# Round counts as one bit mask and one maximum, and the late expert rounds as one loop over the groups, in a two-layer encoder kernel

## The chip, the core and the metric

The kernel runs on one core of a Trainium2 chip. Its engines are TensorE (PE; its weight loads are PEld), VectorE (DVE), ScalarE (ACT), GpSimd (POOL) and SyncE (SP, which here issues nearly all weight transfers). Each engine has a sequencer of its own (PEq, DVEq, ...) that fetches its instructions, takes its branches, and loads its registers. The metric is the device time of one execution in microseconds (us).

## What is computed

Two layers. Each mixes 256 tokens of width 1024 through three branches and one output projection, normalises, and then sends every token to two of 32 experts:

```
x = layer_norm(alpha * x + merged @ w_out[l])
lg = x @ w_rg + b_rg                       # 4 expert groups: the best one
le_sel = the 8 expert logits of that group # the best two experts
h = silu(x @ w_gate_e) * (x @ w_up_e)      # per expert, D_EXPERT = 256
moe_out = (h * weights) @ w_down_e
x = layer_norm(alpha * x + moe_out)
```

How many tokens an expert gets is known only at run time: 16 on the average, and more or less by the data.

## The kernel before, in words

**Stages.** In each layer the mixer comes first: large products whose fp32 weights are split in two (lines 335 and 336), with TensorE busy nearly throughout. Then comes the router, a chain of small DVE and ACT operations, and then the experts. Layer 0's experts run from about 292 to 496 us of the profile, layer 1's from about 785 to 996 us.

**Experts.** The 32 experts are worked in NG = 8 groups of four; this is a grouping of the kernel, not the router's. Each expert has 32 columns of a group's 128, so a group's first round takes up to 32 tokens of each of its experts. For each group `g`, `pick` and `gather` bring the tokens into `xs` by products with a selection matrix `M.S`, eight `columns` steps multiply by the gate and up weights (one 1 MB unit `("gu", l, g, k)` each), and `hidden`, `turn` and four more `columns` steps (`("dn", l, g, k)`) follow. `combine` adds the result to four accumulators.

**More tokens than 32.** Inside the group loop a second round stands under `tc.If(nrv[g] > 0)`: three such branches in group 0 and two in the others around the gate and up products (line 1421), and two around the down products (line 1465), 33 in a layer. An `If` whose condition is false is a branch over its body and a small wait on each engine. Third and later rounds, for an expert with over 64 tokens, stand in `last_rounds` (line 1307), which group 5 calls after its second `columns` step (line 1412). It holds `more_rounds` written out eight times, once for each group, each with a loop over that group's rounds, and all under one `tc.If(nrv[NG] > 1)` (line 1310). In this execution no expert has over 64 tokens, so that branch passes over everything in both layers. In layer 1 groups 2 and 3 have an expert with over 32 tokens and run their second rounds; in layer 0 no group does.

**Counts.** `rounds` (line 1316) turns the counts in `rb_[:, 64:96]` into nine numbers of further rounds, one per group and one over all, by a scale, a rounding by adding and subtracting MAGIC, and a cast to int32. `values_load_multi_w_load_instructions` (line 1392) then has every engine load the nine into registers, with one TENSOR_LOAD. On PE it stands between the last of the WARM = 5 rows of products with zeros (four accumulators each, which start the accumulators and keep the engine at work) and the gather of group 0.

**Weights.** Weight units go through rings of buffers (`Stream`): about 23 units of 1 MB fit ahead. A unit's buffer is given back by `st.done`, in program order, and SP issues the next transfer into it once the engines are past the last use. So transfers stop when all rings are full, and go on when the first group's products give back buffers.

Of the kernel before, what the change touches and what calls it, by code (L numbers as in the profile page):

```python
# [10 lines left out]
F32 = mybir.dt.float32  # L11
F32R = mybir.dt.float32r
BF16 = mybir.dt.bfloat16
I32 = mybir.dt.int32
# [10 lines left out]
NG = 8  # L25
# [169 lines left out]
def emit(nc, tc, dram, out):  # L195
    from contextlib import ExitStack
    ctx = ExitStack()
    with ctx:
# [116 lines left out]
        V.tensor_scalar(ramp[:, 0], iota[:, :64], -1.0, 65.0, op0=OP.mult, op1=OP.add)  # L315
        magic = cp.tile([128, 1], F32, name="magic")
        V.memset(magic, MAGIC)
        hpi = cp.tile([128, 1], F32, name="hpi")
        V.memset(hpi, math.pi / 2)

# [160 lines left out]
        for l in range(L):  # L481
# [685 lines left out]
            e32 = rt([2, 2])  # L1167
            V.tensor_scalar(e32, eid, 32.0, 1.0, op0=OP.mult, op1=OP.add)

            def slots_of(rank, to=None, first=False, beside=lambda: None):  # L1170

                (va, vb, sl), slg = to or ([rt([2, 2]) for _ in range(3)], rt([2, 2, NG]))
                V.tensor_add(va, e32, rank)
                beside()
                if first:
                    V.scalar_tensor_tensor(sl, rank, 32.0, va, op0=OP.is_lt, op1=OP.mult)
                else:
                    V.scalar_tensor_tensor(vb, rank, 32.0, va, op0=OP.is_lt, op1=OP.mult)
                    V.scalar_tensor_tensor(sl, rank, 0.0, vb, op0=OP.is_ge, op1=OP.mult)
                beside()  # L1180
                g128 = iota0[:, 0:NG].unsqueeze(1).to_broadcast([128, 4, NG])
                sl4 = sl.rearrange("p t k -> p (t k)").unsqueeze(2).to_broadcast([128, 4, NG])
                V.scalar_tensor_tensor(slg.rearrange("p t k g -> p (t k) g"), g128, -128.0, sl4, op0=OP.mult, op1=OP.add)
                return slg
# [11 lines left out]
            class X:  # L1196
# [3 lines left out]
                sg, h = l1[:, 0:256], l1[:, 256:512]  # L1200
                hT = cut(sg, [2, 128])
                wv = rt([1])
                rx = rt([2, 2])
                slots = [rt([2, 2]) for _ in range(3)], rt([2, 2, NG])
                bank = pps.tile([128, 512], F32, name="xbank", bufs=1)

# [73 lines left out]
                    for t in range(2):  # L1280
                        mm(accs[t][hf], ST[:, 128 * t:128 * t + 128], yp, False, False)

            def more_rounds(g, y, wf):

                V.tensor_copy(X.rx, rk1)
                with tc.For_i(1, nrv[g], 1):
                    V.tensor_scalar(X.rx, X.rx, -32.0, None, op0=OP.add)
                    pick(g, slots_of(X.rx, X.slots), X)
                    place_back(X, X.bank)
                    for k in (0, 4):  # L1290
                        gather(NG, X.S, X.xs, range(k, k + 4), X.bank)
                    def fetch(src):
                        def w(e):
                            P.dma_start(wf, src[:, 512 * e:512 * e + 512])
                            return wf
                        return w

                    for k in range(8):
                        columns(X.bank, X.xs[k // 4][:, k % 4], fetch(dram["w_gu"][l, g * 8 + k]), k == 0, k == 7)
                    hidden(X.bank, X)  # L1300
                    turn(X, X.bank)
                    for hf in range(2):
                        for f in range(2):
                            columns(X.bank, X.hT[:, f, :], fetch(dram["w_dn"][l, g * 4 + 2 * hf + f]), f == 0, f == 1)
                        combine(X.ST, parts_of(X.bank, y), hf)

            def last_rounds():
                x_rows()
                y = parts_tiles("wl", "wl")
                with tc.If(nrv[NG] > 1):  # L1310
                    for i in range(NG):
                        more_rounds(i, y, l0)

            accs = [[acc_bank() for _ in range(2)] for _ in range(2)]

            def rounds():

                nx = rt([NG + 1])
                V.tensor_reduce(nx[:, :NG], rb_[:, 64:96].rearrange("p (g e) -> p g e", g=NG), axis=AX.X, op=OP.max)
                V.tensor_reduce(nx[:, NG:], rb_[:, 64:96], axis=AX.X, op=OP.max)  # L1320
                yield
                V.tensor_scalar(nx, nx, 1.0 / 32.0, -1.0 / 32.0 - 0.484375, op0=OP.mult, op1=OP.add)
                yield
                V.tensor_scalar(nx, nx, MAGIC, None, op0=OP.add)
                yield
                V.tensor_scalar(nx, nx, MAGIC, 0.0, op0=OP.subtract, op1=OP.max)
                yield
                nxi = rt([NG + 1], I32)
                V.tensor_copy(nxi, nx)
                yield nxi  # L1330

            def weights():
# [47 lines left out]
            with tc.manual_schedule(engines={mybir.EngineType.DVE}):  # L1380

                more = rounds()
                rp = rt([2, 2, 32], t=l1)
                V.tensor_mul(rp, eoh, rb_[:, :64].rearrange("p (t e) -> p t e", t=2).unsqueeze(2).to_broadcast([128, 2, 2, 32]))
                next(more)
                rk = rt([2, 2])
                V.tensor_reduce(rk, rp, axis=AX.X, op=OP.add)
                next(more)
                slg0 = slots_of(rk, first=True, beside=lambda: next(more))
                nxi = next(more)  # L1390
                next(nxt)
                nrv = nc.values_load_multi_w_load_instructions(
                    nxi[0:1, :], min_val=0, max_val=7,
                    skip_runtime_bounds_check_because="an expert has at most 256 tokens, in rounds of 32")[1]
                next(nxt)
                xs = next(nxt)
                rk1 = rt([2, 2])
                V.tensor_scalar(rk1, rk, -32.0, None, op0=OP.add)
                slg1 = slots_of(rk1)
                for _ in wts:  # L1400
                    pass
            for g in range(NG):
                hb = ps_bank()
                for ks in ((0,), (1, 2, 3), (4, 5, 6, 7)) if g == 0 else ((0, 1, 2, 3), (4, 5, 6, 7)):
# [13 lines left out]
                        x_rows()  # L1418
                    if 0 in ks or 7 in ks:
                        xb = ps_bank()  # L1420
                    with tc.If(nrv[g] > 0):
                        if 0 in ks:
                            pick(g, slg1, X)
                            gather(g, X.S, X.xs, range(4), xb)
                            gather(g, X.S, X.xs, range(4, 8), X.bank)
                        for k in ks:
                            columns(X.bank, X.xs[k // 4][:, k % 4], W[k], k == 0, k == 7)
                        if 7 in ks:
                            place_back(X, xb)
                            hidden(X.bank, X)  # L1430
# [21 lines left out]
                for hf in range(2):  # L1452
# [9 lines left out]
                    y = parts_of(yb, y4[hf])  # L1462
                    if g == NG - 1 and hf == 1 and l + 1 == L:
                        last_sums(0)
                    with tc.If(nrv[g] > 0):  # L1465
                        if hf == 0:
                            turn(X, X.bank)
                        for f in range(2):
                            columns(X.bank, X.hT[:, f, :], W[f], f == 0, f == 1)
                        combine(X.ST, parts_of(X.bank, y4[1 - hf]), hf)  # L1470
# [37 lines left out]
```

## Time and profile before

| what | us |
|---|---|
| median of three runs | 1006.58 |
| the three runs | 1005.23, 1006.58, 1011.27 |
| profiled execution, its own time | 1009.82 |
| its span, first to last instruction | 1008.0 |
| PE busy in the span | 892.0 |
| DVE, ACT busy | 577.7, 480.5 |
| instruction fetches, queue q8 | 81 packets, 1.33 MB |

The span is the time between the first and the last recorded instruction; what lies around it is 1.8 us here. A timeline row gives start, duration, engine, line, operation, the tiles written and read, and the count of merged instructions; the bracket at its end is the idle time of the engine just before and what ended it. A product of fp32 data is two weight loads and two products in the trace, so eight `mm` calls show as x16. Register, branch and semaphore instructions are not counted as busy; their durations are seen under the line that issues them.

### The profile page before, as it was taken

Reading aid. Unit: us, or ns where it says so; the run is one execution under the profiler, and the core shown is the slowest. Engines: PE = TensorE matmul, PEld = TensorE weight load, DVE = VectorE, ACT = ScalarE, POOL = GpSimd, SP = SyncE. Lnnn points to the kernel's source line nnn. Section 1 sums busy time; section 2 is a strip of 40 time slices with the busy share of each in tenths; the row PEclk is TensorE's granted clock in tenths of the full one; section 3 lists DMA queues with packets and bytes.
Section 4 is the critical chain, followed back from the end, with each engine's and each line's share of the span. In section 5 each row is a group of like instructions: output and inputs, shape, how many; then the busy total and the mean of one; then the engine's idle time right before and its main releaser. Section 6 shows DMA issues by size and latency. Waiting matters only on the chain. (4 is left out here: it accounts for less than half of the span.)

```text
span 1008.0 us, 19488 instructions
## 1 busy us (share of the span) xinstructions
PE 892.0 (88%) x7718; PEld 662.1 (66%) x7718; DVE 577.7 (57%) x1231; ACT 480.5 (48%) x994; POOL 28.3 (3%) x60
## 2 busy tenths in 40 slices
PE   6899999998989999666797999999899889899793
PEld 6898998988864454212496988998897445444341
DVE  7979798885753212110598998998675331211115
ACT  6876967757532211001389787866664211111112
POOL 3000100000000000001000000000000000000001
PEclk9999999999989999989898999999999989999897
DMA  8573354449759999999984335434788699999991
GB/s 302 214 288 137 101 215 168 169 151 411 315 205 381 418 414 416 412 419 416 354 317 188 98 143 196 184 130 164 282 319 333 235 418 418 418 418 411 414 413 67
DMA packets 48084, 289.06 MB, mean 287 GB/s; under 512 B 5328, under 2 KB 6608, under 8 KB 16080
## 3 DMA queue, kind: packets, MB, share of 16 engines
q1 hardware_dynamic: 47808, 286.26, 72.0%
q8 instruction: 81, 1.33, 0.5%
q10 hardware_dynamic: 144, 1.05, 0.3%
q14 instruction: 51, 0.42, 0.1%
HBM read 286.24 MB, written 1.05 MB: 285 GB/s over the span
## 5 line engine op out<-in xcount | busy, mean ns | idle before, releaser
L336 DVE TENSOR_TENSOR wl<-ringA,wh 128x512 fp32r<-128x512 f32 x280 | 190.0, 692 | 58.5 <-ACT wh L335 55.1
L335 ACT ACTIVATE wh<-ringA 128x512 fp32r<-128x512 f32 x280 | 170.7, 629 | 91.1 <-PE acc L215 76.4
L215 PE MATMUL acc<-xh,wh 128*128 128x256 f32 x576 | 168.6, 295 | 11.7 <-ACT wh L335 11.7
L215 PE MATMUL acc<-xh,wl 128*128 128x256 f32 x576 | 168.0, 292 | 6.1 <-DVE wl L336 5.8
L215 PE MATMUL acc<-xl,wh 128*128 128x256 f32 x576 | 166.7, 290 | 0.0
L215 PEld LDWEIGHTS acc<-xh,wh 128*128 128x128 f32 x576 | 113.2, 198 | 14.6 <-ACT wh L335 12.8
L215 PEld LDWEIGHTS acc<-xh,wl 128*128 128x128 f32 x576 | 113.8, 198 | 8.4 <-DVE wl L336 7.1
L215 PEld LDWEIGHTS acc<-xl,wh 128*128 128x128 f32 x576 | 113.5, 197 | 0.5 <-issue 0.4
L215 PEld LDWEIGHTS ps<-late,xt 128*128 128x128 f32 x544 | 69.8, 208 | 26.6 <-issue 22.0
L215 PE MATMUL ps<-late,xt 128*128 128x128 f32 x544 | 74.4, 295 | 13.7 <-issue 5.9
L215 PE MATMUL acc<-yh,wh 128*128 128x256 f32 x224 | 65.1, 293 | 7.2 <-ACT yh L1038 5.4
L215 PE MATMUL acc<-yh,wl 128*128 128x256 f32 x224 | 64.3, 288 | 0.9 <-DVE wl L336 0.9
L215 PE MATMUL acc<-yl,wh 128*128 128x256 f32 x224 | 64.0, 288 | 0.0
L1275 DVE TENSOR_TENSOR y<-ps,y 128x512 fp32r<-128x512 f32 x32 | 22.1, 692 | 62.1 <-ACTq L1465 51.5
L1274 ACT ACTIVATE y<-ps 128x512 fp32r<-128x512 f32 x32 | 19.1, 598 | 79.7 <-PE ps L215 75.9
L1219 ACT ACTIVATE late<-ps 128x256 fp32r<-128x256 f32 x18 | 6.9, 383 | 99.6 <-PE ps L215 99.6
L215 PEld LDWEIGHTS acc<-y,late 128*128 128x128 f32 x144 | 24.3, 192 | 42.1 <-issue 24.8
L215 PE MATMUL acc<-y,late 128*128 128x512 f32 x144 | 45.6, 432 | 5.8 <-ACT y L1274 3.7
L215 PEld LDWEIGHTS acc<-yh,wh 128*128 128x128 f32 x224 | 43.0, 193 | 9.7 <-ACT yh L1038 5.8
L1209 DVE TENSOR_TENSOR late<-ri,late 128x512 bf16<-128x512 f32 x18 | 12.4, 690 | 64.3 <-PE ps L215 64.1
L215 PE MATMUL ps<-ringA,xs 128*32 128x512 f32 x256 | 34.6, 655 | 14.4 <-PEq L1310 7.6
L215 PEld LDWEIGHTS acc<-yh,wl 128*128 128x128 f32 x224 | 43.4, 194 | 1.6 <-DVE wl L336 1.5
(405 smaller groups left out, 1696.5 us busy)
## 6 DMA issues: line engine op xcount, KB each, us to landing
e<-w_gu SPq DMA_DIRECT2D x34, 1024.0 KB, 9.3
ringB<-w_gu SPq DMA_DIRECT2D x32, 1024.0 KB, 16.7
ringA<-w_gu SPq DMA_DIRECT2D x32, 1024.0 KB, 15.6
ringB<-w_dn SPq DMA_DIRECT2D x31, 1024.0 KB, 16.5
ringA<-w_gate SPq DMA_DIRECT2D x24, 1024.0 KB, 4.9
e<-w_dn SPq DMA_DIRECT2D x23, 1024.0 KB, 12.6
ringA<-w_in SPq DMA_DIRECT2D x15, 1024.0 KB, 4.8
ringA<-w_br SPq DMA_DIRECT2D x12, 1024.0 KB, 4.8
```

The costliest lines, as they stand in the source:

```text
L215: PE.matmul(o, lhsT, rhs, start=start, stop=stop, skip_group_check=True)
L335: A.activation(wh, w, AF.Copy)
L336: V.tensor_sub(wl, w, wh)
L1209: V.tensor_tensor(r.S2, iota.unsqueeze(1).unsqueeze(1).to_broadcast([128, 2, 2, 128]), slg[:, :, :, g].unsqueeze(3).to_broadcast([128, 2, ...
L1219: A.activation(r.ST, b[:, 0:256], AF.Copy)
L1274: A.activation(yh, yb, AF.Copy)
L1275: V.tensor_sub(yl, yb, yh)
```

## The change

Three things, all in the expert stage, and one constant:

- `rounds` makes two numbers in place of nine: `full`, the sum of `1 << g` over the groups with an expert over 32.5 tokens (by a comparison, a product with a constant row `bits`, and a sum), and `most`, the largest count itself. Each engine's TENSOR_LOAD loads two registers.
- The 33 branches of a layer test `full & (1 << g)`, which is one register operation more on each engine ahead of each branch.
- `last_rounds` holds the body once: a loop over the eight groups with the weight addresses taken from the loop's register, and in it a loop over the rounds, whose limit comes from `most`. The slots of the group are reached by moving `X.e`, a copy of `e32`, down by 128 after each group.
- `bits` is filled by eight one-column memsets at the start of the kernel.

WARM is 5 in both kernels. The heart of the diff:

```
-                nx = rt([NG + 1])
-                V.tensor_reduce(nx[:, :NG], rb_[:, 64:96].rearrange("p (g e) -> p g e", g=NG), axis=AX.X, op=OP.max)
-                V.tensor_reduce(nx[:, NG:], rb_[:, 64:96], axis=AX.X, op=OP.max)
+                nx, gx = rt([2]), rt([NG])
+                V.tensor_reduce(gx, rb_[:, 64:96].rearrange("p (g e) -> p g e", g=NG), axis=AX.X, op=OP.max)
+                V.tensor_reduce(nx[:, 1:2], rb_[:, 64:96], axis=AX.X, op=OP.max)
                 yield
-                V.tensor_scalar(nx, nx, 1.0 / 32.0, -1.0 / 32.0 - 0.484375, op0=OP.mult, op1=OP.add)
+                V.scalar_tensor_tensor(gx, gx, 32.5, bits, op0=OP.is_gt, op1=OP.mult)
                 yield
-                V.tensor_scalar(nx, nx, MAGIC, None, op0=OP.add)
+                V.tensor_reduce(nx[:, 0:1], gx, axis=AX.X, op=OP.add)
                 yield
-                V.tensor_scalar(nx, nx, MAGIC, 0.0, op0=OP.subtract, op1=OP.max)
+                nxi = rt([2], I32)
+                V.tensor_copy(nxi, nx)
                 yield
-                nxi = rt([NG + 1], I32)
-                V.tensor_copy(nxi, nx)
                 yield nxi
...
-                nrv = nc.values_load_multi_w_load_instructions(
-                    nxi[0:1, :], min_val=0, max_val=7,
+                full, most = nc.values_load_multi_w_load_instructions(
+                    nxi[0:1, :], min_val=0, max_val=256,
...
-                    with tc.If(nrv[g] > 0):
+                    with tc.If(full & (1 << g)):
...
-                with tc.If(nrv[NG] > 1):
-                    for i in range(NG):
-                        more_rounds(i, y, l0)
+                with tc.If(most > 64):
+                    V.tensor_copy(X.e, e32)
+                    with tc.For_i(0, NG, 1) as g:
+                        V.tensor_copy(X.rx, rk1)
+                        with tc.For_i(1, ((most + 31) >> 5) - 1, 1):
+                            V.tensor_scalar(X.rx, X.rx, -32.0, None, op0=OP.add)
+                            pick(0, slots_of(X.rx, X.slots, e=X.e), X)
...
+                        V.tensor_scalar(X.e, X.e, -128.0, None, op0=OP.add)
```

On DVE, layer 0, between the first use of the rank products and the gather matrix (`late` is the scratch tile that holds the counts, the slots and `M.S`), the program before has

```order
L1387 TENSOR_REDUCE late<-late 128x4
L1322 TENSOR_SCALAR late<-late 128x9
L1173 TENSOR_TENSOR late<-late 128x4
L1324 TENSOR_SCALAR late<-late 128x9
L1176 SCALAR_TENSOR_TENSOR late<-late 128x4
L1326 TENSOR_SCALAR late<-late 128x9
L1183 SCALAR_TENSOR_TENSOR late<-ri,late 128x32
L1329 CAST late<-late 128x9
L1209 TENSOR_TENSOR late<-ri,late 128x512
L1211 TENSOR_TENSOR late<-late 128x256
L1392 TENSOR_LOAD late
```

and the changed program, at the same place, has

```order
L1391 TENSOR_REDUCE late<-late 128x4
L1327 SCALAR_TENSOR_TENSOR late<-late,bits 128x8
L1177 TENSOR_TENSOR late<-late 128x4
L1329 TENSOR_REDUCE late<-late 128x1
L1180 SCALAR_TENSOR_TENSOR late<-late 128x4
L1332 CAST late<-late 128x2
L1187 SCALAR_TENSOR_TENSOR late<-ri,late 128x32
L1213 TENSOR_TENSOR late<-ri,late 128x512
L1215 TENSOR_TENSOR late<-late 128x256
L1396 TENSOR_LOAD late
```

One operation fewer stands there, and the cast that the register loads wait for comes one pair earlier, ahead of the slots' last operation; the two that make `M.S` stay behind that one.

On PE, at the call of `last_rounds` in group 5, the program before goes on like this, the rows from L1286 to the next L1286 being repeated eight times:

```order
L1310 COMPARE_AND_BRANCH
L1286 COMPARE_AND_BRANCH
L1286 UNCONDITIONAL_BRANCH x2
L177 BRANCH_PREFETCH_HINT
L1216 MATMUL xbank<-ident,late 128x128 x2
```

and the changed program has, with the body in it once:

```order
L1298 COMPARE_AND_BRANCH
L1300 COMPARE_AND_BRANCH
L1300 UNCONDITIONAL_BRANCH x2
L177 BRANCH_PREFETCH_HINT
L1302 REGISTER_ALU x3
L1302 COMPARE_AND_BRANCH
L1302 UNCONDITIONAL_BRANCH x2
L177 BRANCH_PREFETCH_HINT
L1220 MATMUL xbank<-ident,late 128x128 x2
```

Seven of the eight bodies are gone between the branch and its target. Counted in the two built programs, with four instructions to a product of fp32 data as in the trace, PE has 24,874 instructions before and 20,598 after, and the branch passes over 2,514 before and 343 after.

## Rows read from the trace of the kernel before

**Rows 1.** The page's head, and its row on instruction fetches (queue: packets, MB).

```profile
span 1008.0 us, 19488 instructions
...
q8 instruction: 81, 1.33, 0.5%
```

**Rows 2.** Busy time by stretch: us, PE, PEld, DVE, ACT, POOL, PEclk, DMA share, GB/s.

```profile
290.00:300.00 10.00, 7.47 (x40) 6.29 (x40) 2.40 (x11) 1.26 (x3) 0.00 (x0) 0.66 0.16 44
300.00:310.00 10.00, 9.53 (x87) 4.79 (x86) 3.29 (x13) 1.62 (x5) 0.00 (x0) 1.00 0.77 305
...
780.00:790.00 10.00, 6.82 (x42) 5.14 (x41) 3.36 (x18) 3.74 (x11) 0.00 (x0) 0.83 0.32 116
...
980.00:990.00 10.00, 8.19 (x76) 2.61 (x72) 0.64 (x2) 3.07 (x6) 0.00 (x0) 1.00 0.44 179
```

**Rows 3.** Timeline of all engines, layer 0's router and first group.

```profile
289.15 0.17 DVE L1329 CAST late<-late 128x9 int32<-128x9 f32 x1
...
290.00 0.42 DVE L1211 TENSOR_TENSOR late<-late 128x256 fp32r<-128x256 bf16 x1
...
291.93 5.46 PE L215 MATMUL ps<-late,xt 128*128 128x128 f32 x24 [3.02 <-issue]
...
298.70 0.33 SPq L157 DMA_DIRECT2D e<-w_dn  x1
```

**Rows 4.** The same place in layer 1.

```profile
782.86 0.42 DVE L1211 TENSOR_TENSOR late<-late 128x256 fp32r<-128x256 bf16 x1
...
784.63 4.41 PE L215 MATMUL ps<-late,xt 128*128 128x128 f32 x24 [2.85 <-issue]
```

**Rows 5.** PE's register loads at line 1392: count, ns min/median/max, first and last start.

```profile
L1392 PEldq TENSOR_LOAD <-late x2: 2193/2275/2357, 289.4 to 782.2; - x2
```

**Rows 6.** PE timeline of layer 0 around the branch of line 1310, and near the layer's end.

```profile
410.10 3.48 PE L215 MATMUL ps<-ringA,xs 128*32 128x512 f32 x16 [4.31 <-PEq L1310]
...
415.87 1.92 PE L215 MATMUL ps<-ringA,xs 128*32 128x512 f32 x16 [1.75 <-issue]
...
420.12 1.07 PE L215 MATMUL ps<-ringD,xs 128*32 128x512 f32 x8 [1.46 <-DMA ringD<-w_gu]
...
488.40 1.57 PE L215 MATMUL ps<-e,late 128*32 128x512 f32 x8 [1.44 <-DMA e<-w_dn]
```

**Rows 7.** PE timeline of layer 1: a plain group, the branch of line 1310, the end.

```profile
912.56 1.19 PE L215 MATMUL acc<-y,late 128*128 128x512 f32 x4
...
920.16 2.02 PE L215 MATMUL ps<-late,xt 128*128 128x128 f32 x16 [0.32 <-PEq L1421]
...
931.57 1.19 PE L215 MATMUL acc<-y,late 128*128 128x512 f32 x4
936.03 3.56 PE L215 MATMUL ps<-ringA,xs 128*32 128x512 f32 x16 [3.27 <-PEq L1310]
...
941.61 0.19 PE L215 MATMUL ps<-late 128*128 128x3 bf16 x2 [1.62 <-issue]
...
943.22 3.42 PE L215 MATMUL ps<-ringD,xs 128*32 128x512 f32 x16
...
948.02 2.02 PE L215 MATMUL ps<-late,xt 128*128 128x128 f32 x16 [0.53 <-ACT late L1258]
...
991.89 1.06 PE L215 MATMUL ps<-e,late 128*32 128x512 f32 x8
```

**Rows 8.** What PE's weight loads waited for on transfers, 780 to 1008 us: total, times, longest.

```profile
PEld ps L215 <- DMA ringB<-w_dn: 0.6, 1, 0.6
...
PEld ps L215 <- DMA e<-w_dn: 0.3, 1, 0.3
```

**Rows 9.** PE's branches by line: count, ns min/median/max, first and last start.

```profile
L1310 PEldq COMPARE_BRANCH  x2: 6017/6168/6319, 403.6 to 929.8; - x2
...
L1421 PEldq COMPARE_BRANCH  x38: 70/223/4460, 296.2 to 983.0; - x38
...
L1465 PEldq COMPARE_BRANCH  x36: 73/210/422, 311.5 to 991.1; - x36
```

More of the change, by code (lines that the diff above doesn't have):

```diff
@@ L317, in emit @@
         V.memset(magic, MAGIC)
+        bits = cp.tile([128, NG], F32, name="bits")
+        for g in range(NG):
+            V.memset(bits[:, g:g + 1], float(1 << g))
         hpi = cp.tile([128, 1], F32, name="hpi")
@@ L1168, in emit, with slots_of @@
             V.tensor_scalar(e32, eid, 32.0, 1.0, op0=OP.mult, op1=OP.add)
-            def slots_of(rank, to=None, first=False, beside=lambda: None):
+            def slots_of(rank, to=None, first=False, beside=lambda: None, e=e32):
                 (va, vb, sl), slg = to or ([rt([2, 2]) for _ in range(3)], rt([2, 2, NG]))
-                V.tensor_add(va, e32, rank)
+                V.tensor_add(va, e, rank)
                 beside()
@@ L1202, in emit @@
                 wv = rt([1])
-                rx = rt([2, 2])
+                rx, e = rt([2, 2]), rt([2, 2])
                 slots = [rt([2, 2]) for _ in range(3)], rt([2, 2, NG])
@@ L1281, in combine @@
                         mm(accs[t][hf], ST[:, 128 * t:128 * t + 128], yp, False, False)
[L1283 to L1305, printed above, removed]
@@ L1307, in last_rounds, with fetch, w @@
             def last_rounds():
                 x_rows()
-                y = parts_tiles("wl", "wl")
-                with tc.If(nrv[NG] > 1):
-                    for i in range(NG):
-                        more_rounds(i, y, l0)
+                y, wf = parts_tiles("wl", "wl"), l0
+                def fetch(src):
+                    def w(e):
+                        P.dma_start(wf, src[:, 512 * e:512 * e + 512])
+                        return wf
+                    return w
+                with tc.If(most > 64):
[5 more added lines that the diff above has]
+                            pick(0, slots_of(X.rx, X.slots, e=X.e), X)
+                            place_back(X, X.bank)
+                            for k in (0, 4):
+                                gather(NG, X.S, X.xs, range(k, k + 4), X.bank)
+                            for k in range(8):
+                                columns(X.bank, X.xs[k // 4][:, k % 4], fetch(dram["w_gu"][l, g * 8 + k]), k == 0, k == 7)
+                            hidden(X.bank, X)
+                            turn(X, X.bank)
+                            for hf in range(2):
+                                for f in range(2):
+                                    columns(X.bank, X.hT[:, f, :], fetch(dram["w_dn"][l, g * 4 + 2 * hf + f]), f == 0, f == 1)
+                                combine(X.ST, parts_of(X.bank, y), hf)
+                        V.tensor_scalar(X.e, X.e, -128.0, None, op0=OP.add)
@@ L1391, in emit @@
                 next(nxt)
-                nrv = nc.values_load_multi_w_load_instructions(
-                    nxi[0:1, :], min_val=0, max_val=7,
-                    skip_runtime_bounds_check_because="an expert has at most 256 tokens, in rounds of 32")[1]
+                full, most = nc.values_load_multi_w_load_instructions(
+                    nxi[0:1, :], min_val=0, max_val=256,
+                    skip_runtime_bounds_check_because="there are eight groups, and an expert has at most 256 tokens")[1]
                 next(nxt)
@@ L1464, in emit @@
                         last_sums(0)
-                    with tc.If(nrv[g] > 0):
+                    with tc.If(full & (1 << g)):
                         if hf == 0:
```

## The prediction

> **What bounds the kernel now.** I read the page's head, then the busy time by stretch, to find where each engine and the transfers go idle; then the timeline at those places; then the register loads and branches by line. The profiled execution took 1009.82 us, 1.8 around a span of 1008.0 [rows 1] and 3.24 over the median of 1006.58. I make the sum as a difference and take it from both.
>
> The change touches only the expert stages. Each opens with a hole: from 290 to 300 us the transfers fall to a 0.16 share and from 780 to 790 to 0.32, and in just these stretches TensorE's granted clock averages 0.66 and 0.83 [rows 2]. The rings are full there, and nothing is given back before the first group's products. Layer 0 goes on transferring only when SP issues at 298.70 [rows 3].
>
> After the hole the layers differ. In layer 0 PE catches up with its weights: it waits for one at 420.12 (1.46 us), and still at 488.40 (1.44 us) [rows 6]. So layer 0's end is set by transfers, which run without a gap once restarted: a gain ahead of the restart reaches the end whole, and a PE stall in mid-layer costs nothing. In layer 1 PE, which also runs second rounds there, waits for a transfer 0.6 and 0.3 us in all [rows 8]. The transfers end near 984.4 (a 0.44 share of 980 to 990 [rows 2]), while the last down weights, which come ahead of one more 1 MB unit (about 2.5 us at the rate of these stages), are used at 991.89 [rows 7]. So there PE is the bound, about 10 us behind its last weights, and a PE stall counts in full, until some 9 us are saved.
>
> **The register loads.** PE's load of nine takes 2.19 to 2.36 us [rows 5]. In layer 0 it starts at 289.4, after the cast, and the gather starts at 291.93; its matrix `M.S` is there at 290.00 + 0.42 = 290.42 [rows 3]. So the load, not the matrix, holds PE. Two registers instead of nine: between 2/9 of 2.28, or 0.51 us, if time goes by the register, and 2.28 if it is one fixed trip. I take the first: at 0.25 us each, nine reads done one after another fit. The load then ends near 289.8 and the matrix becomes the late one, which the order leaves where it was. With 0.05 us for the hand-over the gather starts at 290.47, a gain of 1.46; in layer 1 at 782.86 + 0.42 + 0.05 = 783.33 instead of 784.63 [rows 4], a gain of 1.30. Together **2.8 us**. At the other bound only the missing DVE operation remains, at most the 0.17 of a cast per layer: 0.3. DVE's, ACT's and SP's loads shrink too, behind PE's, where nothing waits for them.
>
> [...]
>
> **The clock.** The gather's 24 products took 5.46 us in layer 0 and 4.41 in layer 1 [rows 3, 4]; 16 such products at full clock take 2.02 [rows 7], so 24 take 3.03. [...] The idle time shrinks to about 1.5 us. After an idle of 1.75 at 415.87 sixteen products ran at full speed, in 1.92 [rows 6]; after one of 1.62 at 941.61 the next sixteen took 3.42 [rows 7]. The rows point both ways, so between 0 and 2.43 + 1.38 = 3.8 I take the middle, **1.9 us**.
>
> **The jump over the late rounds.** PE's branch at line 1310 takes 6.0 to 6.3 us, the others by line 0.2 at the median [rows 9]. In layer 0 this is free, as shown. In layer 1, from the `combine` at 931.57 to the next gather at 948.02, PE needs 16.45 us; in the plain group before, from 912.56 to 920.16, it needs 7.60 [rows 7]. The jump thus costs 8.85 us: 3.27 idle, 1.64 because the next 16 products take 3.56 rather than 1.92 [rows 6, 7], and the rest, 3.9, in an aftermath without a branch: 1.62 idle at 941.61 and a second slow stretch at 943.22.
>
> Is it the length of the jump? Queue q8 fetched 81 packets of 1.33 MB, 16.4 KB each [rows 1]. PE's stream, 24,874 instructions less twice the 2,514 passed over, is 19,846, so about 67 bytes each: I read 256 instructions of 64 bytes to a packet. The idle times at 415.87 and 941.61 stand at no branch; I read them as packet borders whose packet was late. Between them the built program counts 12,281 instructions, 48 packets less 7: good to one per written loop. Counted from these borders in the changed program, layer 0's jump leaves at instruction 136 of a packet and lands at about 481, inside the next one, which was fetched ahead. Layer 1's leaves at 178 and lands at 523: 11 beyond the next packet. So I take the 6 us stall to **stay in layer 1** and vanish only in layer 0, where it was free. But layer 1 then lands at a packet's start, with some 245 instructions to run while the next is fetched, where before it landed near a packet's end. The aftermath goes, a gain of **3.9 us**. Bounds: 0, if the aftermath repeats too; 8.85, if the jump costs what short ones do.
>
> [...]
>
> **What costs nothing.** A layer has 33 more register operations on PE, one per `If`; bounds: nothing, and the shortest PE branch, 70 ns [rows 9], which makes 2.3 us in layer 1. I take nothing: PE's sequencer runs ahead of its products, so far that a 4.46 us stall at a line-1421 branch [rows 9] left 0.53 idle [rows 7]. Without that cover it is the 2.3. The eight one-column memsets stand ahead of the first input's arrival on DVE. The warm-up rows are five in both.
>
> **Sum.** 2.8 + 1.9 + 3.9 = 8.6 us: 1009.82 becomes 1001.2 under the profiler, and the median 1006.58 becomes **998.0 us**.
>
> **The rivals.** *A: the jump is short everywhere.* Layer 1 also keeps the 4.9 us of idle and slow products: 993.1. For it speaks that 343 is nearer to the 43 to 135 instructions of the other `If`s than to 2,514; against it the count, which has to be off by 11.
>
> *B: the load is one fixed trip.* Gains 0.3, no shorter idle, so no clock: 0.3 + 3.9 = 4.2, or 1002.4. Nothing in the rows speaks against it, as both loads seen are of nine.
>
> *C, on the other side: the shifted code brings packets late at other branches.* Every `If` after the change lies elsewhere in its packet, and a branch into a packet still on its way has cost up to 4.46 us [rows 9]. Where it shows on PE as the long jump does (3.27 + 1.64 = 4.9 us), one makes 1002.9, two make 1007.8, slower than before; two is the point from which it decides, and over 1% slower takes four. For it: 66 branches move. Against it: at all of line 1465's branches the stall stayed within 0.42 us [rows 9], and only PE's in layer 1 count.
>
> *D: nothing of it reaches the end.* If layer 0's gain were eaten by a later wait, 998.0 plus 2.4 (its 1.46 and half the clock term), 1000.4; the transfers' full load after the hole speaks against it.
>
> **How the numbers follow.** The forecast has 0.55: with the clock's bounds 6.7 to 10.5 us gained, 996.1 to 999.9. A has 0.18 (991.2 to 995.0 with the same bounds), B 0.12, C 0.08 (0.05 with one, 0.03 with more), D 0.07. From 992.0 to 1003.0 about 0.9 of this lies inside, its top being B or one late packet, and some 0.8 once a cause that I have not named is allowed for. A measurement of this kernel tells some 1% from no change, here 10.1 us, or 996.5. Faster by over 1%: A and the forecast's fast edge, where the clock holds in both layers, 0.28. Slower by over 1% needs four late packets, 0.03. Within 1%: 0.69.
>
> **What would show it.** PE's TENSOR_LOAD near 0.5 us, and the gather ended by DVE's `M.S` with about 1.5 us of idle ahead: the first term. Gathers of 24 products between 3.0 and 5.5 us: the second. PE's branch at the new line 1298 near 0.3 in layer 0 and near 6 us in layer 1, with no further idle at a packet border in group 5: the third; near 0.3 in both is A. I am wrong if PE's load stays at 2 us, if layer 0's end does not move with its first group, or if PE idles 3 us at an `If` of layer 1.

## The result, and the profile after

The changed kernel takes **996.6 us** (median; 995.22 to 999.33) against 1006.3 for the kernel before (1005.23 to 1011.27). The ratio is 0.9878, with a 95% interval of 0.9847 to 0.9908: 1.2% faster. 998.0 was forecast, with 992 to 1003 as the range. A second measurement of the same kernel gave 0.9902 (0.9872 to 0.9932), so the gain is 1.0 to 1.2%.

The profiled execution took 995.22 us. The page's head and its row of instruction fetches [rows 1], then busy time by stretch [rows 2]:

```profile
span 993.6 us, 19826 instructions
...
q8 instruction: 80, 1.31, 0.5%
```

```profile
290.00:300.00 10.00, 7.58 (x66) 4.56 (x64) 5.30 (x26) 2.70 (x6) 0.00 (x0) 1.00 0.54 186
...
780.00:790.00 10.00, 9.09 (x81) 5.07 (x84) 4.78 (x21) 2.11 (x5) 0.00 (x0) 1.00 0.39 116
970.00:980.00 10.00, 7.06 (x52) 2.05 (x44) 3.72 (x7) 3.54 (x6) 0.00 (x0) 1.00 0.72 296
```

In both router stages the granted clock, third from the end, is now 1.00 where it was 0.66 and 0.83. In single microseconds from 292 to 297 us it was 0.50 before: the lower clock of what follows. The timeline of layer 0's router [rows 3] and of layer 1's [rows 4], with the last warm-up products ahead:

```profile
289.07 1.17 PE L215 MATMUL acc<-zeros 128*128 128x512 f32 x4
...
290.25 0.16 DVE L1332 CAST late<-late 128x2 int32<-128x2 f32 x1
...
291.32 0.42 DVE L1215 TENSOR_TENSOR late<-late 128x256 fp32r<-128x256 bf16 x1
...
291.89 2.92 PE L215 MATMUL ps<-late,xt 128*128 128x128 f32 x24 [1.66 <-DVE late L1215]
...
295.95 0.33 SPq L157 DMA_DIRECT2D e<-w_dn  x1
```

```profile
776.81 1.17 PE L215 MATMUL acc<-zeros 128*128 128x512 f32 x4
...
779.06 0.42 DVE L1215 TENSOR_TENSOR late<-late 128x256 fp32r<-128x256 bf16 x1
...
779.63 2.92 PE L215 MATMUL ps<-late,xt 128*128 128x128 f32 x24 [1.65 <-DVE late L1215]
```

PE no longer waits for its own load (`issue`) but for the matrix of line 1215, and the 24 products take 2.92 us in both layers. PE's loads [rows 5] and its branches and register operations by line [rows 9]:

```profile
L1396 PEldq TENSOR_LOAD <-late x2: 554/638/722, 290.4 to 778.2; - x2
```

```profile
L1298 PEldq COMPARE_BRANCH  x2: 325/3166/6006, 401.3 to 920.5; - x2
...
L1425 PEldq COMPARE_BRANCH  x38: 74/224/2913, 294.6 to 968.4; - x38
L1425 PEldq ALU_OP  x34: 36/36/42, 294.5 to 968.3; - x34
```

The jump over the late rounds takes 0.33 us in layer 0 and still 6.01 in layer 1. PE's timeline there, and at the layer's end [rows 7]:

```profile
922.31 1.20 PE L215 MATMUL acc<-y,late 128*128 128x512 f32 x4
926.79 1.92 PE L215 MATMUL ps<-ringA,xs 128*32 128x512 f32 x16 [3.28 <-PEq L1298]
...
933.33 2.02 PE L215 MATMUL ps<-late,xt 128*128 128x128 f32 x16 [0.38 <-PEq L1425]
```

```profile
975.31 1.07 PE L215 MATMUL ps<-e,late 128*32 128x512 f32 x8 [0.40 <-DMA e<-w_dn]
...
977.78 1.07 PE L215 MATMUL ps<-e,late 128*32 128x512 f32 x8 [0.28 <-DMA e<-w_dn]
```

From the `combine` ahead of the jump to the next gather PE needs 11.02 us instead of 16.45, and at the end it now waits for its last down weights. Before, it used them at 991.89, 7.6 us after they had landed (at 984.3).

The spans differ by 14.4 us, more than the medians do. Followed through both timelines, after against before:

- the last warm-up products of layer 0's router start 1.33 us **later** (a stretch at the lower clock near 232 us that the trace of before does not have);
- layer 0's gather starts 1.37 us earlier after them, and takes 2.54 less;
- from there to layer 1's router it is 1.2 us less;
- layer 1's gather starts 1.20 us earlier after its warm-up products, and takes 1.49 less;
- from there to PE's last product it is 7.96 us less, of which the stretch at the jump is 5.43.

About 3 us of the rest of the last item are the same products at the lower clock in the trace of before and at the full one in this; the first of them, in PE's timeline of before, then of after:

```profile
820.91 3.75 PE L215 MATMUL ps<-late,xt 128*128 128x128 f32 x16 [3.16 <-DVE late L1211]
```

```profile
814.41 2.02 PE L215 MATMUL ps<-late,xt 128*128 128x128 f32 x16 [2.92 <-DVE late L1215]
```

### The profile page after: what moved, and what is told of

Its sections match the earlier page's. It is cut to its first block, busy times and chain, and to the rows that moved or that the text cites. A ratio compares the mean times of both kernels' runs of the same rounds, so it can differ in the third digit from the quotient of the medians.

```text
span 993.6 us, 19826 instructions
## 1 busy us (share of the span) xinstructions
PE 882.3 (89%) x7718; PEld 656.0 (66%) x7718; DVE 577.9 (58%) x1237; ACT 480.9 (48%) x994; POOL 28.3 (3%) x60
## 5 line engine op out<-in xcount | busy, mean ns | idle before, releaser
L215 PEld LDWEIGHTS ps<-late,xt 128*128 128x128 f32 x544 | 66.0, 198 | 25.1 <-issue 16.3
L215 PE MATMUL ps<-late,xt 128*128 128x128 f32 x544 | 70.4, 284 | 11.3 <-DVE late L1215 6.2
L215 PEld LDWEIGHTS acc<-yl,wh 128*128 128x128 f32 x224 | 43.8, 196 | 0.1
```

What stands on the lines that cost most here:

```text
L215: PE.matmul(o, lhsT, rhs, start=start, stop=stop, skip_group_check=True)
```

## The experiments

The registers and the loop were tried apart, then the jump's landing, the idle time ahead of the gathers, and the price of a register. "The stretch" below is always PE's time in layer 1 from the start of the `combine` ahead of the late rounds to the start of the next gather; "before" is 16.45.

**The two registers alone.** The written copies are back:

```
-                    with tc.For_i(0, NG, 1) as g:
+                    for g in range(NG):
                         with tc.For_i(1, ((most + 31) >> 5) - 1, 1):
```

> The change without its loop: two registers, but the late rounds written eight times, so that PE passes over 2,517 instructions again instead of 343. Theory (what a jump costs is set by where it lands in its packet): the gain of the load and of the gather's clock stays, 1.38 + 2.54 us in layer 0 and 1.20 + 1.49 in layer 1; the branch at the jump still takes about 6 us in both layers, but in layer 1 it lands 19 instructions into a packet instead of 215 into one, so the second idle time of 1.6 us and the second slow stretch behind it are gone all the same, and from the products before the jump to the second gather behind it PE needs 11 to 13 us as in the changed kernel, not 16.45. In all 995 to 997 us. Rival (the length of what is passed over counts): the stretch takes 16.45 again, only 6.6 us of gain remain: 999.7 us.

Measured: 0.9917 (0.9885 to 0.9948), median 999.8. PE's timeline at the jump of layer 1:

```profile
924.01 1.20 PE L215 MATMUL acc<-y,late 128*128 128x512 f32 x4
928.53 3.64 PE L215 MATMUL ps<-ringA,xs 128*32 128x512 f32 x16 [3.32 <-PEq L1298]
...
937.50 2.02 PE L215 MATMUL ps<-late,xt 128*128 128x128 f32 x16 [0.40 <-PEq L1422]
```

The trace goes with the theory: 2,517 instructions are passed over, and still the second idle time of 1.62 us and the second slow stretch [rows 7] are gone; the stretch takes 13.49. The time decides nothing: against 1006.3 the theory's 995 to 997 us are ratios of 0.989 to 0.991 and the rival's 999.7 is 0.993, and the interval holds them all, as it does the 0.9902 of the changed kernel's second measurement. Nor is the gain the registers' alone: 0.83% is 8.4 us, and the shorter stretch, which came without the loop, is 3 of them in this trace. In layer 0 the branch took 6.23 us again, and from SP's restart to layer 1's register load went 482.1 us, as with the short jump (482.2): there the stall is free.

**The loop alone.** A load of nine words again, the late rounds written once:

```
-                nxi = rt([2], I32)
+                nxi = rt([NG + 1], I32)
```

> The change without its short load: late rounds written once, but the register load again of nine words (seven of them are zeros that nobody reads). PE's instructions stand exactly where they stand in the changed kernel, so the jump of layer 1 leaves and lands at the same places. Theory: PE's load takes 2.3 us again, PE is idle some 2.8 to 3.0 us ahead of both gathers, and their 24 products take 5.4 and 4.4 us instead of 2.92; the stretch at the jump of layer 1 stays at 11.0. In all 996.6 + 6.6 = 1003 us, less what waits at transfers in the end anyway: 1001 to 1003.5. Rival (the gain of the gather came with the shorter code, not with the load): gathers at 2.92 and 997 us.

Measured: 0.9961 (0.9945 to 0.9978). The gathers of layer 0 and layer 1:

```profile
294.38 5.46 PE L215 MATMUL ps<-late,xt 128*128 128x128 f32 x24 [2.80 <-issue]
```

```profile
786.56 2.92 PE L215 MATMUL ps<-late,xt 128*128 128x128 f32 x24 [2.63 <-issue]
```

The ratio is where the expectation had it (against 1006.3, 1001 to 1003.5 us are 0.995 to 0.997). The idle times are as expected; the first gather went at the lower clock, the second, behind 2.63 us of idle, at the full one. So the clock has chance in it, and one gather of one trace decides nothing. The stretch took 12.95 us, where 11.0 was expected. The two halves give 0.83% and 0.39%, the whole 1.0 to 1.2%; but they are no sum of two parts, since the shorter stretch at the jump is in both.

**No late rounds at all.** The call of `last_rounds` is left out.

> The change, with the late rounds left out altogether (on these inputs no expert needs them): no jump at line 1298 at all. Two things differ. If PE is still the bound in layer 1, the 3.4 us that the jump still costs there (11.02 us against the 7.60 of a plain group) come off: 993 us. If the transfers have become the bound (in the changed kernel PE waits 0.40 and 0.28 us for the last down weights), nothing is gained beyond about half a microsecond: 996 to 997 us, with longer waits of PE for transfers in the last two groups of layer 1. I expect the second.

Measured: 0.9886 (0.9856 to 0.9915), 996.5 us. The stretch is 7.66 us, and nothing is gained in time. The end of layer 1:

```profile
973.56 1.07 PE L215 MATMUL ps<-e,late 128*32 128x512 f32 x8 [0.23 <-DMA e<-w_dn]
975.88 1.07 PE L215 MATMUL ps<-e,late 128*32 128x512 f32 x8 [1.25 <-DMA e<-w_dn]
...
978.35 1.06 PE L215 MATMUL ps<-e,late 128*32 128x512 f32 x8 [0.28 <-DMA e<-w_dn]
```

PE waits 1.25 us for one weight where the changed kernel waited 0.40. Its last product ends 1.6 us after the layer's last transfer, against 9.5 in the kernel before and 1.7 and 4.0 in two traces of the changed one. With PE waiting for weights, what is saved at the jump beyond that is waited out. In layer 1, as in layer 0, the transfers are the bound now, or nearly.

**The changed kernel again.**

> The changed kernel once more, to see what of its trace is steady: the ratio to the kernel before between 0.985 and 0.991 again. If the load and the idle time set the gather's clock, both gathers take 2.9 us again with 1.6 us of idle ahead. The stretch at full or lower clock elsewhere (1.3 us lost at 234 us, 3.1 gained at 820 us against the kernel before) may come and go: if it is chance, one of the two is not there this time.

Measured: 0.9902. The gather of layer 1 took 2.92 us again, that of layer 0 4.54, behind the same 1.65 us of idle. The lower clock near 232 us was there (0.59 granted from 232 to 236 us), that near 820 was not. The stretch took 13.60 us: 3.58 us of idle (3.27 before), and 16 products at the lower clock behind it (3.64). The first profile's 11.02 was the lucky one. PE's timeline at the gather of layer 0, then at the jump of layer 1:

```profile
292.92 4.54 PE L215 MATMUL ps<-late,xt 128*128 128x128 f32 x24 [1.65 <-DVE late L1215]
```

```profile
929.92 3.64 PE L215 MATMUL ps<-ringA,xs 128*32 128x512 f32 x16 [3.58 <-PEq L1298]
```

**Where the jump lands.** Products are left out of the body that never runs, so that the landing moves by a few instructions; first one, then five (`DROP` = 4, 3, then 2, 1 of four):

```
-                                combine(X.ST, parts_of(X.bank, y), hf)
+                                combine(X.ST, parts_of(X.bank, y), hf, DROP[hf])
```

> The changed kernel with one product less in the body of the late rounds (one of the eight of their combines is left out; the body does not run on these inputs): two PE instructions less in each layer, 341 passed over. By the count of packets layer 1's jump then lands 7 instructions beyond the next packet, where the changed kernel lands 11 beyond. Theory (the landing's packet decides): PE's branch in layer 1 takes about 6 us as before, and the stretch from the products ahead of the jump to the next gather 11 to 13.6 us; layer 0's branch stays at 0.33. Rival (the stall has another cause than the packet): the same here, so this run is only read beside the next one.

> The same with five of the eight combines of the late rounds' body left out: ten PE instructions less, near enough 334 passed over, and layer 1's jump lands 7 instructions inside the next packet. Theory: the branch takes 0.3 us in layer 1 too, the stretch falls to 7.7 us, as without late rounds, and in the end PE is 1.6 to 2 us behind the transfers instead of 4. Rival (343 and 334 instructions are the same to the branch): 6 us and 11 to 13.6 us as in the run with two less.

PE's branches of the two runs, one execution each:

```profile
L1299 PEldq COMPARE_BRANCH  x2: 334/3188/6043, 402.3 to 923.5; - x2
```

```profile
L1299 PEldq COMPARE_BRANCH  x2: 334/466/597, 403.6 to 923.1; - x2
```

6.04 us with the landing 7 instructions beyond the next packet, 0.60 with it 7 inside. The count of packets holds at this border to within 14 instructions. But the stretch fell only to 11.53, not to 7.7, and here the expectation was wrong. PE's timeline of the second run shows why:

```profile
924.86 1.20 PE L216 MATMUL acc<-y,late 128*128 128x512 f32 x4
926.21 1.02 PE L216 MATMUL ps<-ringA,xs 128*32 128x512 f32 x3
929.79 1.91 PE L216 MATMUL ps<-ringA,xs 128*32 128x512 f32 x13 [2.57 <-issue]
```

After three products PE reaches, by the count, the end of the packet in which it landed, and waits 2.57 us without a branch. The next packet comes only now: queue q8 moves none between 922.3, ahead of the branch, and 927.08, 3.4 us after the landing. That is the idle time of the kernel before at 941.61 [rows 7] over again. The stall had moved, not gone.

The traces also give its size. From the moment at which PE goes on in one packet (here the branch's end, 923.69) to the first instruction of the next packet, where that one is late (here 929.79), it is 6.1 us here, and 5.7 to 6.3 us in all late packets behind these jumps but one (3.7, one group earlier with six rows). In the kernel before it is 5.8 us (935.82 to 941.61). So what shows as idle time is these 6 us less what PE still finds to do in the packet where it landed.

**The late rounds' code one group earlier.** `if g == NG - 4: last_rounds()`; the landing is then at instruction 178 of its packet.

> The changed kernel with the whole of its late rounds, but with their code put one group earlier (group 4 instead of 5). Nothing is left out. By the count of packets the jumps then land at instruction 392 and 434 from the start of the packet that they leave, inside the next one in both layers. Theory: 0.3 us at both branches, the stretch at the jump 7.7 us instead of 11.0 to 13.6, and PE 1.6 to 2 us behind the transfers at the end of layer 1; as without late rounds, a ratio near 0.987 to the kernel before and about 995 to 997 us, 1 to 2 us less than the changed kernel. Rival (moving the code only moves the late packet to another branch): a branch of 3 us or more elsewhere in layer 1 and no gain, 998.

Measured: 0.9872 (0.9843 to 0.9900). The branches took 3.83 us in layer 0, where 0.3 was expected, and 0.45 in layer 1. The stretch took 8.67, and behind its end PE idled once more without a branch:

```profile
909.82 3.64 PE L215 MATMUL ps<-ringB,xs 128*32 128x512 f32 x32 [0.99 <-PEq L1425]
...
915.33 1.50 PE L215 MATMUL ps<-late,xt 128*128 128x128 f32 x12 [0.86 <-issue]
```

So the rival was right in part: late packets moved elsewhere. The next `If` of layer 1 waited 2.99 us for its packet, that of layer 0 5.30, and the 0.86 us is one more; all three ended 5.7 to 5.9 us after PE had gone on in the packet before. That would explain the 3.83 too, though no run tests it: by the count, this jump leaves its packet some 50 instructions from the start, when the next one may still be on its way. On PE the waits cost little, and layer 0's are free: from SP's restart to layer 1's register load it is 482.3 us. In time the kernel cannot be told from the changed one, as the end at the transfers lets one expect.

**The landing moved in the kernel before.** Nine registers, eight copies, three of four products left out of each `combine` in the bodies:

```
-                        combine(X.ST, parts_of(X.bank, y), hf)
+                        combine(X.ST, parts_of(X.bank, y), hf, 1)
```

> The kernel before, nine registers and eight written copies, with six of the eight combines of each copy's body left out (the bodies do not run on these inputs): 2,426 instructions are passed over instead of 2,514. By the count of packets layer 1's jump then lands 39 instructions into a packet instead of 215, and layer 0's 245 into one instead of 77. Theory (the landing decides what follows the jump): the branches still take about 6 us in both layers, but in layer 1 the idle time of 1.6 us and the slow products behind it are gone: the stretch takes 12 to 13.6 us instead of 16.45, and PE is 5 to 7 us behind the transfers at the end instead of 9.5: 3 to 4 us less, a ratio of 0.996 to 0.997, with no other part of the change in it. Rival (the number of instructions passed over counts): 2,426 is as good as 2,514, the stretch stays at 16 and the ratio at 1.000.

```profile
929.92 1.19 PE L215 MATMUL acc<-y,late 128*128 128x512 f32 x4
934.61 3.64 PE L215 MATMUL ps<-ringA,xs 128*32 128x512 f32 x16 [3.50 <-PEq L1310]
...
943.70 2.02 PE L215 MATMUL ps<-late,xt 128*128 128x128 f32 x16 [0.41 <-PEq L1421]
```

The stretch took 13.78 us with 2,426 instructions passed over: 2.67 us less, nearly all of the 2.85 that the changed kernel gains there in its second profile and half of the 5.43 in its first, with no line of the change in it. On the time it is unclear: 0.9985 (0.9962 to 1.0008), where 0.996 to 0.997 was expected; 2.67 us would be 0.997, inside the interval, and so is no gain at all.

**The idle time ahead of the gather.** The kernel before with six rows (`WARM = 6`):

> The kernel before with six rows of warm-up products instead of five, and nothing else: in both layers one more row of four products stands between the counts and the register load of nine, which stays. Theory (the idle time ahead of the gather brings the lower clock, the load only as far as it makes PE idle): the load takes 2.3 us and ends as before, since the row runs beside it; PE is idle 1.85 us instead of 3.02 ahead of the first gather, and the 24 products take 2.9 to 4.5 us instead of 5.46 and 4.41. About 2 to 4 us less: 1003 to 1005 us. Rival (the row delays the load, or the load itself brings the lower clock): the gathers stay at 5.4 and 4.4, 1006 to 1008. The first 230 us hold no difference to the kernel before: if the changed kernels' 1.3 us at 232 us come with their eight memsets, they are absent here.

```profile
294.82 4.54 PE L215 MATMUL ps<-late,xt 128*128 128x128 f32 x24 [2.13 <-issue]
```

```profile
788.45 2.92 PE L215 MATMUL ps<-late,xt 128*128 128x128 f32 x24 [1.96 <-issue]
```

Both gathers are shorter, and SP's first transfer goes out 8.3 and 6.5 us after the loads' start instead of 9.3 and 8.1. But the ratio is 1.001 (0.999 to 1.003). Its trace shows a stretch at the jump of 17.95 us, 1.5 more than before: the added instructions move the landing nearer to its packet's end, and after 8 products and 9 weight loads (so near 239 of 256) PE waits for the next one:

```profile
943.49 1.94 PE L215 MATMUL ps<-ringA,xs 128*32 128x512 f32 x8 [3.86 <-issue]
```

It also shows more stretches at the lower clock in the stages between; whether these two ate the 2.6 us in all its runs is open. The stretch at 232 us is at the lower clock here as well (0.50 granted from 232 to 236 us), without the memsets: they are not its cause.

And the changed kernel with four rows (`WARM = 4`):

> The changed kernel with four rows of warm-up products instead of five: the row between the counts and the load of two is gone, PE is idle some 2.8 us ahead of the gathers instead of 1.65, the matrix comes when it came. (Eight instructions less in each layer also bring layer 1's jump into the next packet: branch 0.3 us.) Theory (the idle time decides the clock, but with chance in it: 1.65 us gave full clock in 13 of 15 gathers of the changed kernels so far, 2.6 to 3.0 us the lower one in 3 of 4): the gather takes 4.4 to 5.5 us in at least one of the layers. What that is worth in all is the question, since six rows in the kernel before gained nothing: if the stage's loss reaches the end, 2.5 and 1.5 us come on top, less 1.5 for the short jump: 999 to 1001 us. If the clock lost here is got back elsewhere, as the six rows suggest, 996 to 998.

```profile
290.56 4.46 PE L215 MATMUL ps<-late,xt 128*128 128x128 f32 x24 [2.67 <-DVE late L1215]
```

```profile
780.93 5.46 PE L215 MATMUL ps<-late,xt 128*128 128x128 f32 x24 [2.67 <-DVE late L1215]
```

Ratio 0.9934 (0.9911 to 0.9958): 3 to 6 us lost against the changed kernel. The load is the short one, and only a row of products ahead of the gather is gone, so here the lower clock came with the idle time of 2.67 us instead of 1.65, and not with the load. The loss is not the clock's alone: the two gathers take 4.1 us more than in the first profile of the changed kernel, and the stretch at the jump, 14.43, is 0.8 and 3.4 more than in its two. (The branch of layer 1 takes 0.88 us, but lands 5 instructions ahead of its packet's end: 2.91 us of idle there, as above.) The count in the expectation was off by one: 12 of 14 gathers.

**The price of a register.** Five words in layer 0, seven in layer 1, one execution.

> The changed kernel with a register load of five words in layer 0 and of seven in layer 1 (the added ones are zeros that nobody reads). Theory (a load takes 0.17 us and 0.234 for each register, a line through 0.64 for two and 2.28 for nine): 1.34 us in layer 0 and 1.81 in layer 1, all within 0.15; in layer 0 the load then ends when the matrix does, and the gather starts as in the changed kernel, in layer 1 the load is the late one by 0.4 us. Rival (two prices, a short and a long one): both near 0.65 or both near 2.3.

```profile
L1398 PEldq TENSOR_LOAD <-late x2: 1423/1584/1745, 290.1 to 781.1; - x2
```

In layer 0 a load of two takes 0.72 us, of five 1.42, of nine 2.36; in layer 1 of two 0.55, of seven 1.75, of nine 2.19. Both are straight lines of 0.23 us for each register, and the other engines pay too: SP's load of nine took 2.07 us in layer 0, of two 0.67. The timeline names the matrix as what ended PE's idle time in both layers, but the matrix had then been there for 0.33 and 0.67 us, against 0.15 in the changed kernel. So the load was the late one in both, in layer 1 as expected. PE stood idle for 1.86 and 2.19 us, and both gathers fell to the lower clock (4.54 and 4.51).

**One group earlier and six rows.**

> The changed kernel with the code of its late rounds one group earlier, as in the run of that kernel, and with six rows of warm-up products instead of five. Nothing is left out; by the count of packets both jumps still land in the next packet (instructions 400 and 450). Theory (idle time ahead of the gather decides its clock): PE's idle ahead of both gathers falls from 1.66 to under 1 us, the matrix stays the late one, and both gathers take 2.92 us, in layer 0 too, where 1.65 us of idle have given 4.54 in two of the seven changed kernels that kept five rows and the load of two. On the mean that is 0.4 us, which no run here tells from nothing: the ratio stays at 0.986 to 0.990, 995 to 998 us. Rival (an added row costs more than it brings, as in the kernel before, where six rows gained nothing although both gathers were faster): the row delays the gather by up to its 1.17 us in each layer, ratio 0.989 to 0.992.

```profile
291.11 2.92 PE L215 MATMUL ps<-late,xt 128*128 128x128 f32 x24 [0.75 <-DVE late L1215]
```

Ratio 0.9864 (0.9840 to 0.9889), with runs between 995.98 and 997.82; layer 1's gather is the same. It is the fastest median of all, but nothing tells it from the changed kernel; the row delays nothing here. Layer 0's jump took 3.84 us again.

All traces together, with the place (of 256) in its packet where layer 1's jump lands. Without a note, that packet lies beyond the next one; the places come from counting instructions, that of the six rows from its trace:

| kernel | gather of layer 0: idle, us | of layer 1 | lands at | stretch |
|---|---|---|---|---|
| before | 3.02, 5.46 | 2.85, 4.41 | 215 | 16.45 |
| before, six rows | 2.13, 4.54 | 1.96, 2.92 | 239 | 17.95 |
| before, shorter bodies | 3.03, 4.40 | 2.87, 4.55 | 39 | 13.78 |
| changed, two profiles | 1.66, 2.92; 1.65, 4.54 | 1.65, 2.92 (both) | 11 | 11.02; 13.60 |
| registers alone | 1.65, 4.54 | 1.65, 2.92 | 19 | 13.49 |
| loop alone | 2.80, 5.46 | 2.63, 2.92 | 11 | 12.95 |
| five and seven words | 1.86, 4.54 | 2.19, 4.51 | 11 | 13.9 |
| one product less | 1.66, 2.92 | 1.65, 2.92 | 7 | 12.5 |
| five products less | 1.66, 2.92 | 1.67, 2.92 | 249, next packet | 11.53 |
| four rows | 2.67, 4.46 | 2.67, 5.46 | 251, next packet | 14.4 |
| one group earlier | 1.66, 2.92 | 1.67, 2.92 | 178, next packet | 8.67 |
| one group earlier, six rows | 0.75, 2.92 | 0.74, 2.92 | 194, next packet | 8.42 |
| no late rounds | 1.66, 2.92 | 1.66, 2.92 | no jump | 7.66 |

## Why the prediction was right

**What bounds.** Right. Layer 0's gain reached the end whole, and a 6.2 us stall in mid-layer cost nothing there. In layer 1 PE was the bound until its lag was used up; without late rounds nothing more was to be had. The stated limit, some 9 us, was about one too high: PE gained 7.8 us on the transfers (9.5 to 1.7) and then stood at its last weights. The reading behind it was off, since the transfers of before end at 986.4 in its trace and not near 984.4, and PE was 7.6 us behind its last down weights and not 10.

**Register loads, 2.8 us.** Right. From the start of the last warm-up products to the gather went 4.19 us before and 2.82 after in layer 0, 4.02 and 2.82 in layer 1: 1.37 and 1.20, in sum 2.57. As forecast the matrix became the late one, and it was there 2.67 us after the start of those products, as before. The 0.2 us that are missing are the hand-over, which took 0.15 us in each layer where 0.05 was allowed. Rival B is out: in these runs the price goes by the register, 0.23 us for each from two (0.72 and 0.55 us) to nine (2.36 and 2.19).

**Clock, 1.9 us.** The mechanism was right, the size a guess between bounds that chance decides. The idle time ahead of the gathers, 3.02 and 2.85 us before [rows 3, 4], came to 1.66 and 1.65, where about 1.5 was forecast. The granted clock, before 0.50 from 291.95 to 297.30 us and 0.63 from 784.65 to 789.00, was 1.00 through both gathers of the first profile. There the clock gave 2.54 + 1.49 = 4.0, just over the upper bound of 3.8, since 24 products take 2.92 at full clock and not 3.03; in the second 0.92 + 1.49 = 2.4. With five rows and two registers 12 of 14 gathers ran at full clock; behind 2.6 to 3.0 us of idle 1 of 8 did.

**The jump, 3.9 us.** The mechanism was right in each part. The stall stayed in layer 1 and vanished in layer 0, PE's branch took 6.01 and 0.33 us, and no second idle time stood behind it. The stretch was forecast at 16.45 − 3.9 = 12.55; with the same landing the four traces have 11.02, 12.95, 13.60 and 13.9, so the gain was 5.4 in one and 2.5 to 3.5 in the others. Most of the difference is the clock again: the 16 products behind the stall took 1.92 us in the first and 3.39 to 3.64 in the rest. Rival A is out, and would not have paid: a landing in the next packet but near its end cost 2.57 and 2.91 us of idle in two runs, and with a good landing the transfers are the bound. That a branch which lands beyond the next packet stalls was the author's reading; two runs show it, on either side of a border that the count has to within 14 instructions: 6.04 us with the landing 7 beyond it, 0.60 with it 7 inside. The 256 instructions of a packet are an estimate, from what queue q8 moved [rows 1] and the count of PE's instructions. And 343 instructions passed over are not short of themselves: that jump still took 6.01 us in layer 1.

**What costs nothing.** Right: PE's register operations take 36 ns each, and its idle time behind plain `If`s stays at 0.3 to 0.4 us (0.38 at 933.33).

**Rivals C and D.** Layer 1 had late packets at other `If`s (2.07, 1.06 and 2.87 us at branches of line 1425 in the first profile), but PE's idle time behind them stayed under 0.4 (0.99 in the worst case of any run), so C's price of 4.9 each was far too high. D is out, since the first profile carried layer 0's gain to the end.

**The sum** of 8.6 stood against 9.7 by the medians and 9.9 to 12.3 by the ratios. The part above it is the clock, at the gathers and behind the jump, and differs from run to run. What this leaves of the 14.4 us between the two spans is luck of the two profiles: 1.3 lost at 232 us, about 3 gained at 820.

## What to carry over

A register load costs by the register here, on every engine that reads it (nine words took 1.90 to 2.36 us, two 0.49 to 0.77), so flags belong in one word, and its worth is what it lets start plus what the shorter idle time does to TensorE's clock (the same 24 products took 5.46 us behind 3.02 us of idle and 2.92 behind 1.66); seven words too many cost 6 to 8 us here, and four warm-up products too few 3 to 6, the shifted jump included. What the jump costs went by where it lands (a branch of 6.04 us with the landing 7 instructions beyond the next packet, of 0.60 with it 7 inside): ask how many instructions are left in the packet before the next is needed (that one came some 6 us after the landing here), and look for the price not only at the branch but as an idle time without one, shortly behind it. Any change in the instructions ahead of a jump moves its landing, so compare the jump too where a run was meant to change something else. And weigh a saving on an engine against its lag behind the transfers: here the lag took up nearly all of it, and the last 3 us or more that the jump still costs (a stretch of 11.02 against 7.66 without it) are worth nothing that can be measured: a ratio of 0.9886 without late rounds, of 0.9878 and 0.9902 with them.

## What the runs showed of the hardware

The lower clock has chance in it even with the same code and the same idle time: behind 1.65 us the same 24 products took 2.92 us in one execution and 4.54 in the next, and behind the same 2.70 us of idle at 228 us the clock fell in the trace of the changed kernel and not in that of before. Busy time from 232 to 236 us, of before and of after (the granted clock is third from the end):

```profile
232.00:236.00 4.00, 4.00 (x36) 4.00 (x36) 3.12 (x7) 3.22 (x7) 0.00 (x0) 1.00 1.03 432
```

```profile
232.00:236.00 4.00, 4.00 (x23) 4.00 (x22) 2.69 (x7) 3.17 (x7) 0.00 (x0) 0.57 1.01 424
```

Such stretches cost 1 to 3 us each and stand in stages that no edit touched, so a profile's span can differ from the median by more than the terms that are looked for.

A short jump can cost nearly as much as a long one: 334 instructions passed over, with the branch at 0.60 us, left PE idle for 2.57 us three products later. A jump that by the count lands well inside the next packet still waited 3.83 us, where it left its own packet some 50 instructions from the start.
